# An encoder block on one core: fp16 parts for the scores, column tiles for the spatial projection, and a later spreading of x's factor

## The chip, the core and the metric

The kernel runs on one core of a Trainium2 chip. Five engines work side by side, each through its own queue in order: TensorE (PE, with the weight loads shown apart as PEld), VectorE (DVE), ScalarE (ACT), GpSimd (POOL) and SyncE (SP), which issues most of the transfers. The metric is the device time of one execution in microseconds. The kernel before takes 721.9 us, the median of three runs (721.56 to 724.05).

## The reference

One layer on 1024 tokens of width 1024, batch 1, all in float32 (cut to what the change touches):

```python
h = rmsnorm(x, norm_gain)
q, k, v, gate_a, u_in, v_in, gate_b, g_merge = jnp.split(h @ w_in, IN_SPLITS, axis=-1)
q = axial_rope(rmsnorm(q.reshape(B, S, 8, 64), q_gain), row_ang, col_ang)   # 8 query heads
k = axial_rope(rmsnorm(k.reshape(B, S, 2, 64), k_gain), row_ang, col_ang)   # 2 key heads
attn = block_attention(q, k, v) * silu(gate_a)      # softmax(q k / 8) v, both directions
u = gelu(u_in)
vv = layernorm(gelu(v_in), ln_v_gain, ln_v_bias).reshape(B, 8, 128, 8, 64)
v_mix = einsum('gij,bcjgd->bcigd', w_spatial, vv) + b_spatial.T[:, :, None]
gm = u * v_mix.reshape(B, S, 512) * silu(gate_b)
g = sigmoid(g_merge + b_merge)
out = rmsnorm(x + (g[0] * (attn @ w_proj_attn) + g[1] * (gm @ w_proj_gmlp)) @ w_out, final_gain)
```

## The kernel before

Every large product is made from split operands: an operand is written as hi + lo, and a product as three matmuls, hi·hi, hi·lo and lo·hi (`mm3`, L181 to L184). Some operands are split into two fp32r halves (`split`, L125 to L127: a copy on ACT, a subtraction on DVE), others are scaled and split into two fp16 halves (`split16`, L291 to L293).

The work goes in stages. First x arrives and k, v and the value half of the gated branch are projected (tiles `kv`, and `v` in four groups of two token blocks, `v_group`). Then, for each of 8 token blocks of 128, the layer norm (`v_post`) and the spatial projection (`spatial`): four slices of 256 columns of w_spatial, each by `mm3` with the block's fp32r halves as the stationary operand, into a PSUM tile `sp`; two copies on ACT (L398) pick out the half of the rows that is wanted for each of the two channel groups of a slice. In between come the query projection (`q_group`, tile `q`), the normalisation and rotation of q and k on DVE (`q_norm`, `rope`), their split into halves (`q_split` into `qs`, `khl` for k) and their transposes on PE (`qtp`, `ktp`), which ACT and DVE copy out of PSUM into `qT` and `kT`. A query block's `qs` holds hi in the first 64 of each 128 values and lo in the other 64, so that one transposed tile holds both halves as rows.

Attention is 64 pieces `scores(j, qt, h)`: four matmuls into a PSUM tile `s` (L626, L627, the query tile is the stationary operand), a row maximum on DVE (`nm`, L629), the exponential on ACT (`P`, L633), a reciprocal, the fp16 halves of the probabilities (`p`, ACT L639 and DVE L640), and a transfer that transposes them into `T`. `mix2` multiplies T by v on two column tiles of 64 (L654, tile `o`): two neighbouring matmuls write the lower and upper 64 rows of the output. Between the pieces stand the projections of u and of the two gates (`run_fill`, tiles `u`, `ga`, `gb`, L560 to L562). After the last piece come the projections `yb` (from `gm`), the merge gates `g`, the projections `y` and the output product `out`.

`scales` squares and sums a weight block (ACT L344, after a load of 256 KB into one of four buffers `wraw`) to get its scale; the result goes through a small PE product (`us...`), ACT and POOL. The factor 1/rms of x is spread over the partitions by 8 small products (`rb`, L271) and copied to `rB` (L274), which `norm_part` and `x_chunk` use.

The order is set twice: a list at the end of the function, written out as calls, says in which order the steps are recorded; from it a scheduler sets the final order on each engine. PSUM has three buffers for the large tiles (`S`) and one each for `o` and `z`.

Of the kernel before, what the change touches and what calls it, by code (L numbers as in the profile page):

```python
# [30 lines left out]
def hybrid_block_kernel(  # L31
# [342 lines left out]
    def v_post(c):  # L374
# [13 lines left out]

    def spatial(c):
        vh, vl = vhl[c]  # L390
        pt = ps_s(f"sp{c}")
# [4 lines left out]
        for g2 in range(2):
            rows = slice(64 * g2, 64 * g2 + 64)
            act.copy(vm[rows, :, C(c)], p3[rows, :, C(g2)])  # L398

# [37 lines left out]
    def q_split(tt):  # L437
        if True:
            g, k = tt // 2, tt % 2
            q4 = qsts[g].rearrange("p (t h d) -> p t h d", h=8, d=64)  # L440
# [1 line left out]
            act.copy(qs[:, :, 0:64], q4[:, k])
            dve.tensor_tensor(out=qs[:, :, 64:128], in0=q4[:, k], in1=qs[:, :, 0:64].bitcast(F32), op=ALU.subtract)
            full = ps_s(f"qtp{tt}") if QTP[g] == "s" else None
            for hh in range(2):
                if full is not None:
                    pt = full[:, H(hh)]
                else:
                    pt = {"o": ps_o, "z": ps_z, "S": ps_s}[QTP[g][hh]](f"qtp{tt}{hh}")
                for h in range(4):  # L450
                    pe.transpose(pt[:, C(h)].bitcast(F32R), qs[:, 4 * hh + h, :], identr)
# [99 lines left out]
    def v_affine(t):  # L551
        m3 = vm[:, t, :].rearrange("p (c i) -> p c i", i=128)
        dve.scalar_tensor_tensor(out=m3, in0=m3, scalar=cs[:, C_LNG + t:C_LNG + t + 1],
# [437 lines left out]
    load_pair(1)  # L991
    load_wsp(1)
    load_pair(2)
    early = scales(["q"] + order[:4], ["xa"] * 8)
    with tc.high_priority():
        scales_end(*early)
        qc = const([P, 2], "qc")
        dve.tensor_scalar(out=qc[:, 1:2], in0=wsc["q"][1], scalar1=2.0, scalar2=None, op0=ALU.mult)
        dve.tensor_scalar(out=qc[:, 0:1], in0=qc[:, 1:2], scalar1=qc[:, 1:2], scalar2=1.0 / 64, op0=ALU.mult, op1=ALU.mult)
    v_group(2)  # L1000
# [383 lines left out]
```

## Time and profile before

| | before |
|---|---|
| median of 3 runs | 721.9 us |
| the profiled execution | 722.31 us |
| its span, first to last instruction | 720.5 us |
| mean granted TensorE clock | 0.993 |
| PE busy | 696.2 us, 97% |
| DVE busy | 575.5 us, 80% |
| ACT busy | 455.2 us, 63% |
| POOL busy | 117.1 us, 16% |

Busy time of a matmul runs from its start to its modelled end, so neighbouring matmuls overlap; how fast PE takes them is read from the distance of two starts in the timeline. In the rows of the windows, a line gives a stretch of the span, then the busy time of each engine with its instructions, the granted clock (PEclk), the share of the DMA engines and their rate. In the rows of waits, the three numbers are the sum in us, the count and the longest.

### The profile page before, as it was taken

The page shows a single profiled execution, that of the slowest core. Times are in us where ns is not written, and L with a number is a line of the kernel's source. Part 1 is how long each engine was busy: PE and PEld are TensorE (multiplying, and loading weights), DVE is VectorE, ACT ScalarE, POOL GpSimd, SP SyncE. Part 2 cuts the span into 40 slices and gives each one's busy share as a digit, 9 for nine tenths or more (in the row PEclk, how much of TensorE's full clock was granted, in tenths as well). Part 3 has the DMA queues.
Part 4 walks back from the last instruction along what each step waited for, and adds up shares of the span by engine and source line. Part 5 has one row for each costly group of instructions (what it writes and reads, how often), then busy time and mean ns, then how long its engine had stood idle before and what let it go on. Part 6 is the DMA issues. An engine that isn't in the chain of part 4 may idle for free.

```text
span 720.5 us, 11891 instructions
## 1 busy us (share of the span) xinstructions
PE 696.2 (97%) x4625; PEld 461.9 (64%) x4625; DVE 575.5 (80%) x820; ACT 455.2 (63%) x810; POOL 117.1 (16%) x106
## 2 busy tenths in 40 slices
PE   8999999799899999999999999999999999999996
PEld 8888666455466556566656786644464557488885
DVE  6489988789898998988788899978897899953223
ACT  6775796787788977896776577545474544721011
POOL 0024224045020101011100093011012020000000
PEclk9999999999999999999999999999999999999999
DMA  8993244625689996999799630310120125330202
GB/s 295 402 405 117 89 132 134 203 37 110 117 136 189 217 183 128 187 187 178 137 202 206 193 102 15 132 72 3 41 106 1 58 88 176 116 118 12 106 30 87
DMA packets 157512, 98.18 MB, mean 136 GB/s; under 512 B 135952, under 2 KB 136592, under 8 KB 157456
## 3 DMA queue, kind: packets, MB, share of 16 engines
q1 hardware_dynamic: 156016, 92.95, 51.0%
q10 hardware_dynamic: 1440, 4.47, 1.6%
q8 instruction: 36, 0.59, 0.3%
q14 instruction: 20, 0.16, 0.1%
HBM read 59.65 MB, written 4.19 MB: 89 GB/s over the span
## 4 chain that ended last, share of the span: by engine, by line
PE 60%; DVE 14%; DMA 11%; ACT 8%; issue 4%; POOL 1%; SPq 1%; POOLq 0%; ACTq 0%; DVEq 0%
PE out L182 4%; PE out L183 4%; PE out L184 4%; DMA wraw<-in_wall_dram 4%; DMA T<-p 3%; DMA xraw<-in_xT_dram 3%; PE o L654 3%; PE g L182 3%; PE g L184 3%; PE g L183 3%; DVE p L640 3%; DVE nm L629 3%; PE s L626 2%; PE s L627 2%; PE yb L182 1%
## 5 line engine op out<-in xcount | busy, mean ns | idle before, releaser
L640 DVE SCALAR_TENSOR_TENSOR p<-P,ri,p 128x1024 f16<-128x1024 f32 x64 | 83.4, 1306 | 18.6 <-ACT p L639 18.2
L633 ACT ACTIVATE P<-s,nm 128x1024 f32<-128x1024 f32 x64 | 71.1, 1110 | 20.2 <-DVE nm L629 15.4
L639 ACT ACTIVATE p<-P,ri 128x1024 f16<-128x1024 f32 x64 | 73.0, 1142 | 10.8 <-DVE ri L636 5.8
L629 DVE TENSOR_REDUCE nm<-s 128x1 f32<-128x1024 f32 x64 | 77.4, 1212 | 1.2 <-PE s L627 1.1
L626 PE MATMUL s<-kT,qT 128*128 128x512 f32 x128 | 57.2, 447 | 8.2 <-ACT P L633 4.3
L654 PEld LDWEIGHTS <-vS 128*64 128x64 f16 x1536 | 45.1, 110 | 15.4 <-issue 13.1
L654 PE MATMUL o<-T,vS 128*64 128x128 f16 x1536 | 49.9, 220 | 3.7 <-DMA T<-p 3.6
L627 PE MATMUL s<-kT,qT 128*128 128x512 f32 x128 | 51.6, 403 | 0.0
L285 POOL TENSOR_SCALAR scg<-scg 128x1 f32<-128x1 f32 x8 | 18.8, 2348 | 181.1 <-ACT usg L284 181.1
L927 ACT ACTIVATE sq<-xr 128x1024 f32<-128x1024 f32 x7 | 7.4, 1062 | 63.5 <-DVE xr L1314 63.2
L1314 DVE TENSOR_TENSOR xr<-out,xr 128x1024 f32<-128x1024 f32 x7 | 8.6, 1225 | 45.9 <-PE out L184 45.7
L183 PE MATMUL out<-wo,yhl 128*128 128x512 f32 x96 | 37.5, 390 | 0.0
L182 PE MATMUL out<-wo,yhl 128*128 128x512 f32 x96 | 37.4, 392 | 0.0
L184 PE MATMUL out<-wo,yhl 128*128 128x512 f32 x96 | 37.3, 390 | 0.0
L182 PE MATMUL g<-x,wg 128*128 128x512 f16 x96 | 36.4, 379 | 0.0
L184 PE MATMUL g<-x,wg 128*128 128x512 f16 x96 | 36.4, 379 | 0.0
L183 PE MATMUL g<-x,wg 128*128 128x512 f16 x96 | 36.4, 379 | 0.0
L626 PEld LDWEIGHTS s<-kT,qT 128*128 128x128 f32 x128 | 24.8, 194 | 17.2 <-ACT P L633 5.5
L627 PEld LDWEIGHTS s<-kT,qT 128*128 128x128 f32 x128 | 24.9, 195 | 4.5
L182 PE MATMUL yb<-gm,wh 128*128 128x512 f32 x64 | 25.2, 394 | 0.0
L560 PE MATMUL u<-x,wu 128*128 128x512 f16 x64 | 24.3, 380 | 0.9 <-ACT s1b L357 0.6
L182 PE MATMUL v<-nh,xhl 128*128 128x512 f32 x64 | 25.1, 392 | 0.0
(547 smaller groups left out, 2016.1 us busy)
## 6 DMA issues: line engine op xcount, KB each, us to landing
wraw<-in_wall_dram SPq DMA_DIRECT2D x75, 256.0 KB, 3.4
graw<-in_wall_dram SPq DMA_DIRECT2D x16, 512.0 KB, 4.8
xraw<-in_xT_dram SPq DMA_DIRECT2D x13, 512.0 KB, 6.6
xn<-in_x_dram SPq DMA_DIRECT2D x8, 512.0 KB, 7.9
xp<-in_xT_dram SPq DMA_DIRECT2D x8, 512.0 KB, 8.2
xr<-in_x_dram SPq DMA_DIRECT2D x8, 512.0 KB, 3.7
wor<-in_wall_dram SPq DMA_DIRECT2D x8, 512.0 KB, 4.7
out_dram<-xr SPq DMA_DIRECT2D x7, 512.0 KB, 2.6
```

Source lines behind the costliest of these rows:

```text
L182: pe.matmul(o, ah, bh, start=start, stop=False)
L183: pe.matmul(o, ah, bl, start=False, stop=False)
L184: pe.matmul(o, al, bh, start=False, stop=stop)
L285: pool.tensor_scalar(out=sc[:, 1:2], in0=sc[:, 1:2], scalar1=1.0, scalar2=1e-30, op0=ALU.mult, op1=ALU.add)
L560: pe.matmul(o, wh, x16[dt][:, 0, H(h)], start=(dt == 0), stop=False)
L626: pe.matmul(sp[:, H(hf)], qs, kT[v][:, 0, H(hf)], start=True, stop=False)
L627: pe.matmul(sp[:, H(hf)], qs, kT[v][:, 1, H(hf)], start=False, stop=True)
L629: dve.tensor_reduce(out=nm, in_=sp, axis=AX.X, op=ALU.max, negate=True)
L633: act.activation(Pt, sp, AF.Exp, bias=nm, accum_out=rsum)
L639: act.activation(hi, Pt, AF.Copy, scale=ri)
L640: dve.scalar_tensor_tensor(out=lo, in0=Pt, scalar=ri, in1=hi, op0=ALU.mult, op1=ALU.subtract)
L654: pe.matmul(ot[64 * h:64 * h + 64, C(k)], vS[:, kt, v, 64 * vl:64 * vl + 64], T[:, h, 8 * p + kt, :], start=(n == 0), stop=(n == len(parts ...
```

## The change

What it does:

- **Scores.** `qs`, `khl`, `qT` and `kT` become fp16 (hi and lo halves of fp16 each), and the transposes use an fp16 identity and fp16 PSUM tiles. So that q and k lie in the range of fp16, the gains of q and k are rescaled by a common factor, made from their largest values by a few small steps on DVE and one on POOL (`gsz`).
- **Spatial projection.** w_spatial is scaled and split into fp16 halves (`wsw`), with a scale made as for the other weights: ACT squares both halves of it (into `wss`), a small PE product (`uswsp`), an ACT copy, three POOL steps, then `split16`. The normalised block is split into fp16 halves (`vhl`). `spatial` now takes two token blocks at once: for each of them 4 slices x 3 products x 2 channel groups, each with 64 stationary columns and 128 moving ones; the two channel groups are written to the lower and upper 64 rows of the PSUM tile, as in `mix2`. One ACT copy for both blocks takes the place of four. The scale is undone in `v_affine` (`lgs`).
- **Spreading of x's factor.** The products `rb` and their copies to `rB` are recorded after the first `v_group`, without priority, and no longer ahead of it.
- **The list.** Many calls stand in another order. On PE, `rb` still follows the 18 last matmuls of the first `v` group in both kernels, and the sums of the number of large matmuls are the same but for the 96 `sp` matmuls of 256 columns, which become 192 of 128 columns on column tiles.

```diff
-    rB = t4("rB", "rB")
-    with tc.high_priority():
-        rp = [ps_z("rb0"), ps_o("rb1")]
...
-        vh = sb.tile([P, 512], F32R, tag="wh", bufs=3, name=f"vh{c}")
-        vl = sb.tile([P, 512], F32R, tag="wl", bufs=3, name=f"vl{c}")
-        split(vh, vl, g, act)
-        vhl[c] = vh, vl
-
-    def spatial(c):
-        vh, vl = vhl[c]
-        pt = ps_s(f"sp{c}")
-        for t in range(4):
-            r = slice(256 * t, 256 * t + 256)
-            mm3(pt[:, r], vh[:, C(t)], vl[:, C(t)], wsh[:, r], wsl[:, r], True, True)
-        p3 = pt.rearrange("p (k i) -> p k i", k=4)
-        for g2 in range(2):
-            rows = slice(64 * g2, 64 * g2 + 64)
-            act.copy(vm[rows, :, C(c)], p3[rows, :, C(g2)])
+        vhl[c] = sb.tile([P, 2, 512], F16, tag="wh", bufs=3, name=f"vhl{c}")
+        split(vhl[c][:, 0], vhl[c][:, 1], g, act)
+
+    def spatial(k):
+        pt = ps_s(f"sp{k}")
+        for i in range(2):
+            v = vhl[2 * k + i]
+            for t in range(4):
+                for n, (a, b) in enumerate(((0, 0), (0, 1), (1, 0))):
+                    for g2 in range(2):
+                        o = 128 * t + 64 * g2
+                        pe.matmul(pt[64 * g2:64 * g2 + 64, 512 * i + 128 * t:512 * i + 128 * t + 128], v[:, a, o:o + 64],
+                                  wsw[:, b, 2 * 128 * t + 128 * g2:2 * 128 * t + 128 * g2 + 128],
+                                  start=(n == 0), stop=(n == 2))
+        act.copy(vm[:, :, 256 * k:256 * k + 256].rearrange("p t (c i) -> p t c i", c=2),
+                 pt.rearrange("p (c t i) -> p t c i", c=2, t=4))
...
-            qs = t4("og", f"qs{tt}", F32R).rearrange("p (h d) -> p h d", d=128)
+            qs = t4("og", f"qs{tt}", F16).rearrange("p (h d) -> p h d", d=128)
             act.copy(qs[:, :, 0:64], q4[:, k])
-            dve.tensor_tensor(out=qs[:, :, 64:128], in0=q4[:, k], in1=qs[:, :, 0:64].bitcast(F32), op=ALU.subtract)
+            dve.tensor_tensor(out=qs[:, :, 64:128], in0=q4[:, k], in1=qs[:, :, 0:64], op=ALU.subtract)
...
-                    pe.transpose(pt[:, C(h)].bitcast(F32R), qs[:, 4 * hh + h, :], identr)
+                    pe.transpose(pt[:, C(h)], qs[:, 4 * hh + h, :], identh)
...
-        split(wsh[:, H(h)], wsl[:, H(h)], raw, act)
+        act.activation(wsw[:, h].bitcast(F32), raw, AF.Square, accum_out=wss[:, h:h + 1])
+
+    def scale_wsp():
+        nscale.append("wsp")
+        pt = ps_oz(len(nscale), "uswsp")
+        pe.matmul(pt[:, 0:2], mscale.broadcast_to([P, P]), wss, start=True, stop=True)
+        sc = sb.tile([P, 2], F32, tag="sc", bufs=3, name="scwsp")
+        act.activation(pt[:, 8:10], pt[:, 0:2], AF.Copy, accum_out=sc[:, 1:2])
+        pool.tensor_scalar(out=sc[:, 1:2], in0=sc[:, 1:2], scalar1=1.0, scalar2=1e-30, op0=ALU.mult, op1=ALU.add)
+        pool.tensor_tensor(out=sc[:, 0:1], in0=sc[:, 1:2], in1=mhalf[:, 0:1], op=ALU.pow)
+        pool.tensor_tensor(out=sc[:, 1:2], in0=sc[:, 1:2], in1=sc[:, 0:1], op=ALU.mult)
+        for h in range(2):
+            split16(wsw[:, 0, H(h)], wsw[:, 1, H(h)], wsr[h], sc[:, 0:1], "dve")
+        dve.tensor_scalar(out=lgs, in0=cs[:, C_LNG:C_LNG + 4], scalar1=sc[:, 1:2], scalar2=None, op0=ALU.mult)
...
-                pe.transpose(pt[:, C(2 * s + k)].bitcast(F32R), khl[s][:, C(2 * t2k + k)], identr)
+                pe.transpose(pt[:, C(2 * s + k)], khl[s][:, C(2 * t2k + k)], identh)
...
     v_group(0)
+    rB = t4("rB", "rB")
+    rp = [ps_z("rb0"), ps_o("rb1")]
+    for tt in range(NT):
+        pe.matmul(rp[tt // 4][:, C(tt % 4)], rstdh[:, tt:tt + 1].broadcast_to([P, P]), identr.bitcast(F32),
+                  start=True, stop=True)
+    for h in range(2):
+        dve.tensor_copy(rB[:, H(h)], rp[h])
     v_group(1)
...
+    gsz = const([P, 4], "gsz")
+    for i in range(2):
+        dve.tensor_reduce(out=gsz[:, i:i + 1], in_=gq[:, 128 * i:128 * i + 64], axis=AX.X, op=ALU.max,
+                          apply_absolute_value=True)
+    dve.tensor_scalar(out=gsz[:, 2:3], in0=gsz[:, 0:1], scalar1=gsz[:, 1:2], scalar2=1e-30, op0=ALU.mult, op1=ALU.max)
+    pool.tensor_tensor(out=gsz[:, 2:3], in0=gsz[:, 2:3], in1=mhalf[:, 0:1], op=ALU.pow)
...
+    kT4 = sb.tile([P, 4, 1024], F16, tag="X", bufs=8, name="kT")
+    kT = [kT4[:, 2 * v:2 * v + 2] for v in range(2)]
...
+    qT2 = [sb.tile([P, 2, 2, 1024], F16, tag="qT", bufs=4, name=f"qT{i}") for i in range(2)]
+    qT = [qT2[j // 2][:, j % 2] for j in range(4)]
```

**How the built program moves.** Three places follow, each as the built program of the kernel before and of the changed one has it (line, operation, out<-in, shape; "x2" stands for two alike; numbers tell buffers apart).

The first is ACT just ahead of the first copies of transposed queries, without which the first score cannot start. Before:

```order
L442 CAST qs_1242<-qst_1048 128x8x64
L442 CAST qs_1259<-qst_1048 128x8x64
L398 COPY vm<-sp_1414 64x4x128 x2
L344 ACTIVATE wraw_2078,ssa_2075<-wraw_2078 128x512
L344 ACTIVATE wraw_2081,ssa_2075<-wraw_2081 128x512
L344 ACTIVATE wraw_2084,ssa_2075<-wraw_2084 128x512
L344 ACTIVATE wraw_2087,ssa_2075<-wraw_2087 128x512
L344 ACTIVATE wraw_2101,ssb_2098<-wraw_2101 128x512
L344 ACTIVATE wraw_2104,ssb_2098<-wraw_2104 128x512
L344 ACTIVATE wraw_2107,ssb_2098<-wraw_2107 128x512
L344 ACTIVATE wraw_2110,ssb_2098<-wraw_2110 128x512
L453 CAST qT_863<-qtp_1245 128x2x128
```

and in the changed kernel, where L338 is the square, L447 the copy of queries, L392 the copy of `sp`:

```order
L338 ACTIVATE wraw_1953,ssb_1950<-wraw_1953 128x512
L338 ACTIVATE wraw_1956,ssb_1950<-wraw_1956 128x512
L535 COPY qst_1444<-q_1395 128x1024
L447 COPY qT_941<-qtp_1319 128x2x128 x2
L447 COPY qT_942<-qtp_1326 128x2x128 x2
L436 CAST qs_1352<-qst_1065 128x8x64
L338 ACTIVATE wraw_1959,ssb_1950<-wraw_1959 128x512
L338 ACTIVATE wraw_1962,ssb_1950<-wraw_1962 128x512
L338 ACTIVATE wraw_1976,ssa_1973<-wraw_1976 128x512
L392 COPY vm<-sp_1446 128x4x256
L338 ACTIVATE wraw_1979,ssa_1973<-wraw_1979 128x512
L436 CAST qs_1369<-qst_1225 128x8x64
```

Eight squares, each of a freshly loaded weight block, stood ahead of the first copies of queries; now two do. The last copy of `sp`, which stood ahead of the eight, now has five of the squares ahead of it.

The second is DVE around the first row maximum. Before:

```order
L553 SCALAR_TENSOR_TENSOR vm<-vm,cs,bsp 128x1024 x4
L443 TENSOR_TENSOR qs_1322<-qst_1191,qs_1322 128x8x64
L629 TENSOR_REDUCE nm_1485<-s_1480 128x1
L406 TENSOR_REDUCE qf_1657<-qtmp_1655 128x16
L142 TENSOR_SCALAR qf_1657<-qf_1657,qc 128x16
L629 TENSOR_REDUCE nm_1529<-s_1524 128x1
```

and in the changed kernel (L561 is `v_affine`, L437 the query split, L637 the row maximum):

```order
L561 SCALAR_TENSOR_TENSOR vm<-vm,lgs,bsp 128x1024 x4
L437 TENSOR_TENSOR qs_1369<-qst_1225,qs_1369 128x8x64
L437 TENSOR_TENSOR qs_1614<-qst_1225,qs_1614 128x8x64
L637 TENSOR_REDUCE nm_1575<-s_1570 128x1
L400 TENSOR_REDUCE qf_1677<-qtmp_1675 128x16
L637 TENSOR_REDUCE nm_1602<-s_1597 128x1
```

The four `v_affine` steps, which need the last copy of `sp`, stand ahead of the first row maximum in both; one more query split stands there now.

The third is ACT where the scale of w_spatial is taken up, in the changed kernel alone (L485 copies the small product, L286 makes the fp16 halves, L334 squares the blocks of the first scales):

```order
L465 ACTIVATE vst_513<-v_529,rstd 128x512 x2
L485 ACTIVATE uswsp,scwsp<-uswsp 128x2
L286 ACTIVATE wsw<-wspr_601,scwsp 128x512
L286 ACTIVATE wsw<-wspr_647,scwsp 128x512
L286 ACTIVATE x_921<-xp_662,gs 128x1024
L334 ACTIVATE squ_641,ssq<-squ_641 128x1024
L286 ACTIVATE x_944<-xp_662,gs 128x1024
L334 ACTIVATE sqb_644,ssq<-sqb_644 128x1024
```

On POOL the three steps between the second row and the third stand behind the power of 16 values for k (L146 there, L143 before):

```order
L375 TENSOR_SCALAR rs_743<-mv_741 128x1
L375 TENSOR_SCALAR rs_805<-mv_803 128x1
L376 TENSOR_TENSOR rs_743<-rs_743,mhalf 128x1
L376 TENSOR_TENSOR rs_805<-rs_805,mhalf 128x1
L146 TENSOR_TENSOR kf<-kf,mhalf 128x16
L486 TENSOR_SCALAR scwsp<-scwsp 128x1
L487 TENSOR_TENSOR scwsp<-scwsp,mhalf 128x1
```

The two fp16 halves of w_spatial and the squares behind them now wait for POOL; before, the split of w_spatial came some twenty ACT steps earlier and waited for no scale.

More of the change, by code (lines that the diff above doesn't have):

```diff
@@ L21 @@
 PSCALE = 32768.0
+QKMAX = 32768.0
 VSCALE = 16384.0
@@ L473, in hybrid_block_kernel @@
     vhl = {}
-    wsh = t4("og", "wsh", F32R)
-    wsl = t4("og", "wsl", F32R)
+    wsw = t4("og", "wsw", F16, (P, 2048)).rearrange("p (k c) -> p k c", k=2)
+    wss = const([P, 2], "wss")
+    lgs = const([P, 4], "lgs")
     wsr = []
@@ L552, in v_affine @@
         m3 = vm[:, t, :].rearrange("p (c i) -> p c i", i=128)
-        dve.scalar_tensor_tensor(out=m3, in0=m3, scalar=cs[:, C_LNG + t:C_LNG + t + 1],
+        dve.scalar_tensor_tensor(out=m3, in0=m3, scalar=lgs[:, t:t + 1],
                                  in1=bsp[:, None, C(t)].broadcast_to([P, 8, 128]),
@@ L990, in hybrid_block_kernel @@
     Ak, Bk = (heads(t) for t in tabk)
[L991 to L1000, printed above, removed]
+    load_wsp(0)
     v3 = vn.rearrange("p (t e) -> p t e", e=128)
@@ L1007, in hybrid_block_kernel @@
                       apply_absolute_value=True)
-    norm_part(1)
-    prep_q(0)
-    v_group(3)
-    bias_term(0)
-    v_post(1)
-    spatial(1)
-    norm_part(0)
-    prep_q(1)
     ktmp = t4("vS", "ktmp")
     head_norm(kn, ktmp, 0, 8, "kf")
-    prep_q(2)
+    load_pair(1)
+    early = scales(["q"] + order[:4], ["xa"] * 8)
+    load_wsp(1)
+    scale_wsp()
+    load_pair(0)
+    load_pair(2)
+    with tc.high_priority():
+        scales_end(*early)
+        qc = const([P, 2], "qc")
+        dve.tensor_scalar(out=qc[:, 1:2], in0=wsc["q"][1], scalar1=2.0, scalar2=None, op0=ALU.mult)
+        dve.tensor_scalar(out=qc[:, 0:1], in0=qc[:, 1:2], scalar1=qc[:, 1:2], scalar2=1.0 / 64, op0=ALU.mult, op1=ALU.mult)
+    prep_q(0)
+    v_group(2)
+    norm_part(0)
+    v_post(0)
+    v_group(3)
+    v_post(1)
+    prep_q(1)
+    bias_term(0)
+    norm_part(1)
+    norm_part(5)
     with tc.high_priority():
@@ L1102, in hybrid_block_kernel @@
     v_affine(2)
+    scores(*hs[1])
     q_split(3)
-    scores(*hs[1])
     scores(*hs[2])
@@ L1121, in hybrid_block_kernel @@
     v_affine(3)
+    q_split(7)
+    v_affine(1)
     run_fill(*halves[0])
     q_split(6)
-    q_split(7)
+    scales(order[8:10])
+    scales(order[10:12])
     scores(*hs[12])
-    v_affine(1)
+    v_affine(0)
     mix2(*hs[0][:2])
+    scores(*hs[13])
+    scores(*hs[14])
+    prep_next()
     mix2(*hs[4][:2])
-    scales(order[10:12])
-    scales(order[8:10])
-    run_fill(*halves[1])
-    prep_next()
-    scores(*hs[13])
-    v_affine(0)
-    scores(*hs[14])
     prep_next()
@@ L1145, in hybrid_block_kernel @@
     scores(*hs[20])
+    scores(*hs[21])
     prep_next()
-    scores(*hs[21])
     mix2(*hs[12][:2])
@@ L1167, in hybrid_block_kernel @@
     scores(*hs[30])
+    scores(*hs[31])
     run_fill(*halves[11])
-    scores(*hs[31])
+    run_fill(*halves[12])
     scores(*hs[32])
@@ L1172, in hybrid_block_kernel @@
     mix2(*hs[24][:2])
-    run_fill(*halves[12])
     scores(*hs[34])
```

150 lines of the change are left out of this document (73 added, 77 removed).

## The prediction, made before the changed kernel ran

> **What bounds the kernel now.** I read the page first, then the windows stage by stage, then PE's waits, then the timeline where they stand.
>
> ```profile
> PE 696.2 (97%) x4625; PEld 461.9 (64%) x4625; DVE 575.5 (80%) x820; ACT 455.2 (63%) x810; POOL 117.1 (16%) x106
> ...
> 43.40:141.40 98.00, 93.48 (x495) 64.65 (x495) 89.27 (x140) 72.36 (x129) 29.25 (x27) 1.00 0.47 162
> 141.40:247.10 105.70, 98.47 (x871) 62.64 (x872) 94.40 (x130) 87.25 (x168) 25.30 (x20) 0.97 0.72 134
> 247.10:379.40 132.30, 130.37 (x1321) 80.91 (x1320) 113.28 (x144) 105.56 (x184) 13.79 (x10) 1.00 0.95 172
> 379.40:442.00 62.60, 62.43 (x441) 47.08 (x441) 57.88 (x82) 40.57 (x73) 22.06 (x4) 1.00 0.57 147
> 442.00:720.50 278.50, 271.97 (x1239) 170.51 (x1236) 196.55 (x283) 118.47 (x209) 23.76 (x36) 0.99 0.21 74
> ```
>
> The last five rows are A (values and queries, to 141.4), B (first part of attention, to 247.1), C (the rest of it, to 379.4), D (to the first merge gate) and E. PE is the bound in C, D and E (130.37 of 132.30, 62.43 of 62.60). In B it isn't alone: PE is busy 98.47 of 105.70 and DVE 94.40, so a PE that gets shorter by more than some 7 us there meets DVE, and the 0.97 shows a stretch of slower clock. The change's operations lie in A, B and C; D and E keep all their matmuls and start earlier by what the others save.
>
> ```profile
> PE s L626 <- ACT qT L453: 3.9, 1, 3.9
> ...
> 132.32 0.63 ACT L344 ACTIVATE wraw<-wraw 128x512 f32<-128x512 f32 x1
> ...
> 136.33 0.63 ACT L344 ACTIVATE wraw<-wraw 128x512 f32<-128x512 f32 x1 [2.06 <-DMA wraw<-in_wall_dram]
> ...
> 140.30 0.63 ACT L344 ACTIVATE wraw<-wraw 128x512 f32<-128x512 f32 x1 [0.69 <-DMA wraw<-in_wall_dram]
> ...
> 141.05 1.20 ACT L453 CAST qT<-qtp 128x256 fp32r<-128x256 f32 x4
> ...
> 147.72 1.11 ACT L633 ACTIVATE P<-s,nm 128x1024 f32<-128x1024 f32 x1
> ```
>
> The longest wait of PE in attention, 3.9 us before the first score, is not a lack of speed: ACT stands in line behind eight squares of weight blocks, 132.32 to 140.9, of which some wait for transfers; the copies of the transposed queries come only behind them.
>
> ```profile
> 142.49 0.63 PE L626 MATMUL s<-kT,qT 128*128 128x512 f32 x1
> 142.91 0.63 PE L627 MATMUL s<-kT,qT 128*128 128x512 f32 x1
> ...
> 136.97 1.27 DVE L553 SCALAR_TENSOR_TENSOR vm<-vm,cs,bsp 128x1024 f32<-128x1024 f32 x1
> 142.79 0.69 DVE L443 TENSOR_TENSOR qs<-qst,qs 128x512 fp32r<-128x512 f32 x1 [4.54 <-ACT qs L442]
> ...
> 150.01 0.69 DVE L443 TENSOR_TENSOR qs<-qst,qs 128x512 fp32r<-128x512 f32 x1 [2.68 <-ACT qs L442]
> 150.62 0.16 DVE L636 RECIPROCAL ri<-ri 128x1 f32<-128x1 f32 x1
> ```
>
> The same line costs DVE 4.54 and 2.68 us, and the scores right behind PE's wait go at 0.42 us apart. [...]
>
> **The change part by part.** *Scores.*
>
> ```profile
> 263.38 0.38 PE L561 MATMUL u<-x,wu 128*128 128x512 f16 x1
> 263.59 0.38 PE L562 MATMUL u<-x,wu 128*128 128x512 f16 x1
> 263.62 0.58 PE L626 MATMUL s<-kT,qT 128*128 128x512 f32 x1
> 264.04 0.39 PE L627 MATMUL s<-kT,qT 128*128 128x512 f32 x1
> 264.27 0.39 PE L626 MATMUL s<-kT,qT 128*128 128x512 f32 x1
> ...
> 141.40:247.10 105.70, 33.34 (x107) 20.91 (x108) 30.61 (x26) 30.03 (x50) 0.97 0.72 134
> 247.10:379.40 132.30, 38.69 (x145) 26.28 (x144) 43.25 (x37) 43.21 (x72) 1.00 0.95 172
> ```
>
> The last two rows are the windows for tile s alone: 107 of the 256 score matmuls fall into B, 145 into C. An fp16 matmul of 512 columns follows its neighbour after 0.215 us (263.38 to 263.59), a score after 0.23 (264.04 to 264.27): 0.015 saved on each, 1.6 us in B and 2.2 in C. And the first score behind fp16 work holds back the next by 0.42 (263.62 to 264.04), 0.19 more than its share; behind `o` it is 0.34, as in the row of 254.67 below. By the timeline there are some 18 such entries in each of B and C, half behind `o`; at 0.15 on the mean, 2.7 us in each. fp16 behind fp16 shows none of it, so I take both away: 4.3 us in B, 4.9 in C. Bounds: cadence alone (1.6 and 2.2) to all.
>
> *Spatial projection.*
>
> ```profile
> 79.62 0.47 PE L182 MATMUL sp<-wsh,vh 128*128 128x256 f32 x1
> ...
> 82.64 0.39 PE L182 MATMUL q<-wq,x 128*128 128x512 f16 x1
> ...
> 254.67 0.51 PE L626 MATMUL s<-kT,qT 128*128 128x512 f32 x1
> 255.01 0.40 PE L627 MATMUL s<-kT,qT 128*128 128x512 f32 x1
> ...
> 255.49 0.40 PE L627 MATMUL s<-kT,qT 128*128 128x512 f32 x1
> 255.82 2.87 PE L654 MATMUL o<-T,vS 128*64 128x128 f16 x95
> 258.62 0.39 PE L560 MATMUL u<-x,wu 128*128 128x512 f16 x1
> ...
> L398 ACT COPY vm<-sp 64x512 f32<-64x512 f32 x16 | 9.3, 579 | 1.2 <-PE sp L184 1.0
> ```
>
> Two blocks take 24 matmuls from 79.62 to 82.64, 3.0 us; four such pairs 12.1. The new form, 64 stationary and 128 moving columns on two column tiles, is that of `o`: 95 in 2.80 us (255.82 to 258.62), 0.0295 each, so 192 take 5.7. The built order cuts the four bursts into nine pieces; entering one costs 0.33 instead of 0.23, and leaving about as much, so 9 x 0.23 = 2.1. Saved: 12.1 - 7.8 = 4.3 us of PE, in A. [...] Bounds: 5.9 (whole bursts) and, if the pairs did not overlap, 12.1 - 192 x 0.059 - 2.1 = -1.3. Sixteen copies of 0.58 on ACT become four of at most 1.16 (twice the values each): 5 us less on ACT, which is not the bound in A (72.36 of 98).
>
> *Transposes.*
>
> ```profile
> 133.80 0.98 PE L451 MATMUL qtp<-identr,qs 128*128 128x128 f32 x8
> 134.62 0.39 PE L184 MATMUL q<-wq,x 128*128 128x512 f16 x1
> ```
>
> Eight take 0.82, 0.10 each. In fp16 I bound one from above by that, from below by 0.06 (128 columns, a pair of `o`): 0 to 2.6 us for the 64, most in B; I take 1.5. The copies out of them keep their size.
>
> *Scales.* DVE gains the steps of `gsz` and `lgs`, seven or so at about 0.16 (the row of 150.62): 1.1 us. ACT gains two squares, and its two halves of w_spatial now wait for POOL:
>
> ```profile
> 56.42 4.95 POOL L143 TENSOR_TENSOR kf<-kf,mhalf 128x16 f32<-128x16 f32 x1 [6.07 <-DVE kf L142]
> ...
> L356 PE MATMUL usq<-ssq,mscale x8: 173/253/254, 67.4 to 68.1; 128*128 128x5 f32 x8
> L285 POOL TENSOR_SCALAR scg<-scg 128x1 f32<-128x1 f32 x8 | 18.8, 2348 | 181.1 <-ACT usg L284 181.1
> ```
>
> POOL is free at 61.4; its three small steps end at 63 to 65 (a small one lasts up to 2.35). Two halves, two splits of x and the two last squares, at 0.65 to 1.25 each on ACT, then end at 69 to 71, and `usq`, due on PE at some 68.6 (67.4 before, and five matmuls of `v` later in the new order) with 42 matmuls of `v` behind it, waits 0 to 2.5. I take 0.5. The later `rb` costs and saves nothing: it keeps its place on PE.
>
> *The sum.* In A PE ends its queries 4.3 us earlier; the 3.9 us of waiting go too, since only two squares stand ahead of the first copies. But what then sets the pace is DVE: without its 4.54 and 2.68, less 1.1 of new work, the row maxima start 6.1 us earlier at best, and not at all if the last copy of `sp`, now behind five squares, keeps `v_affine` waiting as the queries were kept. It is five squares instead of eight, so nearer the upper end: 4.5, less 0.5 for `usq`, 4.0. In B PE loses 4.3 + 1.5 = 5.8 and DVE has some 7 us of other idle time to give; bounds 0 and 5.8, I take 4, since both would have to be dense for all of it. In C DVE is busy 113.28 of 132.30, so PE's 4.9 pass whole (3 to 4.9). Together 12.9 us: 722.3 (the profiled execution, 1.8 above its span) less 12.9 is 709.4; the median shown is 0.4 below it, so **709 us**.
>
> D can keep what the others give, but not more:
>
> ```profile
> 446.30 0.74 DVE L293 SCALAR_TENSOR_TENSOR wg0T<-s,scg,wg0T 128x512 f16<-128x512 f32 x1
> ...
> 447.18 0.38 PE L182 MATMUL g0T<-x,wg0T 128*128 128x512 f16 x1
> ```
>
> DVE, busy 57.88 of 62.60, finishes a gate's weights at 447.04 and PE uses them at 447.18. If attention ends earlier for PE than for DVE, PE waits here.
>
> **The rivals.** *PE alone counts* (chance 0.20). PE's savings, 4.3 + 3.9 + 5.8 + 4.9, and 2 us of slow clock pass whole: 20.9, so 701. For it: 97% busy. Against: DVE's 94.40 in B and the pair of rows just shown.
>
> *DVE takes the place of the waits* (0.14). The row maxima start no earlier, B stays at its length, only C gives 4.9 less 1.1: 718. For it: DVE ties with PE in B and D. Against: its idle time at 138 to 150 comes from ACT's line alone.
>
> *fp16 or the column tiles don't act as the nearest rows say* (0.04): scores keep their entries and `sp` pairs run one by one; A gives 2, B 2, C 2.2: 715.5.
>
> *Slower: the last copy of `sp`* (0.06). It stands behind five squares that wait for transfers; `v_affine`, 4 x 1.27, two query splits and the first row maximum stand behind it on DVE, and the first exponential behind that. PE, at its first score near 133, runs out of PSUM tiles after three scores and 21 other matmuls (33 at 0.215, near 140) and stands until that exponential. Before, it came at 147.72. From a copy later than about 147, which puts the exponential at 156, this eats all other gains and brings slow clock: 726. Eight squares took 8.5 us before, so five would have to take more than a dozen.
>
> **How the numbers follow.** The forecast's own case, 703 to 716, has 0.56. The range takes in PE alone at its lower end and DVE at its upper one: 699 to 719. A measurement of this kernel can tell about 0.5% from no change, 718.3 to 725.5. Faster: 0.56 + 0.20 + 0.04 + somewhat under half of 0.14, 0.86. Slower: 0.06. Within: 0.08.
>
> **What would show it.** Scores in the profile after at 0.215 with no longer step at entries; `sp` bursts near 0.03 a matmul; the first score at 133 to 136 without a wait for the query copies and without slow clock; A to the last query 4 us shorter; B with DVE over 92% busy; C shorter by 4 to 5. The prediction is wrong if PE shows a new wait of several us in B (for exponentials, or at `usq`), if DVE's idle time in B stays at 11, or if PE waits at the merge gates in D.

## The result, and the profile after

| | before | after |
|---|---|---|
| median of 8 runs each | 722.6 us | 718.0 us (715.6 to 720.1) |
| ratio, with its 95% interval | | 0.993 (0.991 to 0.995) |
| the profiled execution | 722.31 us | 718.27 us |
| its span | 720.5 us | 716.5 us |

The change makes the kernel 0.7% faster, some 4.6 us; the forecast was 13, with a range of 699 to 719. The direction is right, the size a third of it. The lines of the page, after:

```profile
span 716.5 us, 12060 instructions
...
PE 689.4 (96%) x4723; PEld 430.9 (60%) x4723; DVE 575.8 (80%) x828; ACT 450.9 (63%) x804; POOL 103.6 (14%) x110
...
PE 46%; DVE 23%; DMA 12%; ACT 10%; issue 5%; POOL 2%; SPq 1%; POOLq 0%; DVEq 0%; ACTq 0%
```

The last line is the chain that ended last, by engine. The same line of before:

```profile
PE 60%; DVE 14%; DMA 11%; ACT 8%; issue 4%; POOL 1%; SPq 1%; POOLq 0%; ACTq 0%; DVEq 0%
```

PE is still busy 96% of the time, but its share of that chain fell from 60 to 46%, and DVE's rose from 14 to 23. Now the stages, each kernel cut at the same five events: the first score, the first score of piece 33, the first merge gate's product behind the last `yb`, the last gate product (`g7T`), the end. Before, and then after:

```profile
0.00:141.40 141.40, 132.94 (x757) 100.72 (x757) 113.41 (x184) 103.41 (x181) 32.21 (x36) 1.00 0.62 222
141.40:265.60 124.20, 116.97 (x1036) 73.77 (x1037) 111.99 (x151) 102.79 (x195) 27.83 (x22) 0.98 0.77 141
265.60:441.80 176.20, 174.09 (x1595) 116.75 (x1594) 153.37 (x204) 130.38 (x228) 33.31 (x12) 1.00 0.80 162
441.80:628.80 187.00, 187.00 (x866) 100.77 (x866) 163.48 (x245) 102.21 (x185) 19.40 (x28) 1.00 0.21 74
628.80:720.50 91.70, 85.17 (x374) 69.85 (x372) 33.27 (x40) 16.45 (x25) 4.36 (x8) 0.98 0.19 75
```

```profile
0.00:137.80 137.80, 131.32 (x863) 95.47 (x864) 111.65 (x191) 101.92 (x183) 35.59 (x40) 0.99 0.64 229
137.80:258.70 120.90, 112.02 (x1030) 59.54 (x1028) 112.04 (x153) 98.61 (x187) 27.21 (x22) 0.97 0.81 142
258.70:434.30 175.60, 171.81 (x1595) 105.57 (x1593) 152.76 (x201) 130.03 (x227) 20.91 (x12) 1.00 0.80 163
434.30:623.30 189.00, 187.65 (x866) 100.45 (x866) 166.07 (x248) 103.88 (x187) 15.53 (x28) 1.00 0.21 73
623.30:716.50 93.20, 86.61 (x374) 69.84 (x372) 33.33 (x40) 16.44 (x25) 4.37 (x8) 0.98 0.20 73
```

Each stage holds the same products of PE in both kernels, but for a few transposes and small products. The length of the stages changes by -3.6, -3.3, -0.6, +2.0 and +1.5 us. In the second, DVE is now as busy as PE (112.04 and 112.02 of 120.90), with a slightly lower granted clock (0.97, before 0.98). The last two, whose matmuls the change doesn't touch, became longer. PE's waits after:

```profile
PE o L662 <- DMA T<-p: 5.3, 6, 1.9
PE ga L568 <- DVE uw L590: 3.0, 1, 3.0
PE s L634 <- ACT P L641: 2.7, 2, 1.5
PE q L186 <- DVE wq L287: 2.1, 1, 2.1
PE vabT L1050 <- DVE bsp L499: 1.3, 1, 1.3
PE usb L350 <- DVE uw L590: 1.2, 1, 1.2
...
PE g0T L187 <- DVE wg0T L287: 0.9, 2, 0.6
PE y00T L185 <- DVE ya L744: 0.5, 1, 0.5
```

The wait of 3.9 for the query copies is gone. But all rows of this view together make 20.3 us, where before they made 17.6: without that wait, 13.7 became 20.3. The new rows are waits for DVE.

### The profile page after: what moved, and what is told of

It reads as the page before. It is cut to its first block, busy times and chain, and to the rows that moved or that the text cites. A ratio compares the mean times of both kernels' runs of the same rounds, so it can differ in the third digit from the quotient of the medians.

```text
span 716.5 us, 12060 instructions
## 1 busy us (share of the span) xinstructions
PE 689.4 (96%) x4723; PEld 430.9 (60%) x4723; DVE 575.8 (80%) x828; ACT 450.9 (63%) x804; POOL 103.6 (14%) x110
## 4 chain that ended last, share of the span: by engine, by line
PE 46%; DVE 23%; DMA 12%; ACT 10%; issue 5%; POOL 2%; SPq 1%; POOLq 0%; DVEq 0%; ACTq 0%
PE out L187 4%; PE out L185 4%; PE out L186 4%; DMA T<-p 4%; DVE p L648 4%; DMA xraw<-in_xT_dram 4%; DVE nm L637 3%; ACT p L647 3%; PE g L185 3%; PE g L187 3%; PE g L186 3%; DMA wraw<-in_wall_dram 2%; PE o L662 2%; ACT P L641 2%; DMA xn<-in_x_dram 1%
## 5 line engine op out<-in xcount | busy, mean ns | idle before, releaser
L637 DVE TENSOR_REDUCE nm<-s 128x1 f32<-128x1024 f32 x64 | 77.4, 1212 | 1.8 <-PE s L635 1.7
L634 PE MATMUL s<-kT,qT 128*128 128x512 f16 x128 | 48.6, 380 | 2.8 <-ACT P L641 2.7
L635 PE MATMUL s<-kT,qT 128*128 128x512 f16 x128 | 48.5, 379 | 0.0
L279 POOL TENSOR_SCALAR scg<-scg 128x1 f32<-128x1 f32 x8 | 4.6, 581 | 201.3 <-ACT usg L278 161.9
L186 PE MATMUL q<-wq,x 128*128 128x512 f16 x64 | 24.8, 390 | 2.1 <-DVE wq L287 2.1
L186 PE MATMUL yb<-gm,wh 128*128 128x512 f32 x64 | 25.2, 394 | 0.0
L185 PE MATMUL yb<-gm,wh 128*128 128x512 f32 x64 | 25.1, 393 | 0.0
L286 ACT ACTIVATE wg<-graw,scg 128x512 f16<-128x512 f32 x16 | 11.5, 722 | 21.5 <-PE g L187 11.4
```

Of the source, the lines that this page charges most:

```text
L185: pe.matmul(o, ah, bh, start=start, stop=False)
L186: pe.matmul(o, ah, bl, start=False, stop=False)
L286: act.activation(hi, raw, AF.Copy, scale=sc)
L634: pe.matmul(sp[:, H(hf)], qs, kT[v][:, 0, H(hf)], start=True, stop=False)
L635: pe.matmul(sp[:, H(hf)], qs, kT[v][:, 1, H(hf)], start=False, stop=True)
L637: dve.tensor_reduce(out=nm, in_=sp, axis=AX.X, op=ALU.max, negate=True)
```

## Experiments

Theory D: PE's shorter work turns into waits, because DVE (or the chain of a piece through DVE and ACT) sets the pace. Theory P: PE sets it, and the waits are a small rest. The table collects what each run gave: the ratio of its time to the kernel before with its interval, in its profile the start of the last query product, of the first score of piece 33 and of the last `yb` product, and the sum of PE's waits.

| kernel | ratio (95%) | last q | piece 33 | last yb | waits |
|---|---|---|---|---|---|
| before | 1 | 137.2 | 265.7 | 441.6 | 17.6 |
| the change | 0.993 (0.991, 0.995) | 137.7 | 258.8 | 434.1 | 20.3 |
| consts_moved | 0.991 (0.990, 0.993) | 138.1 | 259.9 | 433.8 | 21.0 |
| pe_less_early | 1.000 (0.998, 1.002) | 137.9 | 264.2 | 440.0 | 27.4 |
| pe_less_late | 0.995 (0.993, 0.997) | 139.0 | 258.9 | 433.1 | 22.3 |
| dve_less_early | 0.999 (0.998, 1.001) | 138.8 | 261.9 | 438.4 | 22.5 |
| dve_less_late | 0.999 (0.997, 1.000) | 138.5 | 259.8 | 438.5 | 21.1 |
| old_with_fp16_scores | 1.000 (0.999, 1.001) | 137.0 | 264.7 | 441.0 | 24.7 |
| old_with_fp16_spatial | 1.001 (1.000, 1.002) | 138.9 | 266.1 | 441.4 | 21.7 |
| old_with_both_parts | 0.997 (0.996, 0.998) | 141.8 | 261.7 | 436.2 | 21.3 |
| new_with_fp32r_scores | 1.008 (1.006, 1.011) | 140.2 | 261.7 | 444.8 | 19.6 |
| uw_on_act | 1.002 (1.001, 1.004) | 138.2 | 262.3 | 437.3 | 23.6 |
| rb_mult_on_pool | 0.991 (0.989, 0.993) | 137.5 | 258.2 | 432.1 | 22.9 |
| four_on_pool | 0.999 (0.997, 1.001) | 142.6 | 267.6 | 441.6 | 25.0 |
| both_mends | 0.988 (0.986, 0.990) | | | | |
| both_mends_again | 0.992 (0.990, 0.994) | 138.4 | 258.3 | 432.0 | 22.0 |
| mixes_one_later | 1.000 (0.999, 1.002) | 138.0 | 264.0 | 441.1 | 25.8 |
| vab_in_other_bank | 1.002 (1.001, 1.004) | 144.1 | 266.6 | 441.0 | 26.1 |

The profiled one of both_mends' five executions took 1800.7 us, the other four 712.7 to 714.8, so its places are left empty; both_mends_again is the same kernel.

Each place is from one execution. consts_moved has the instructions of the change in the same order on PE, DVE and ACT, and rb_mult_on_pool those of both_mends_again. Within these two pairs the last query product differs by 0.4 and 0.9, the first product with v by 2.3 and 2.6, piece 33 by 1.1 and 0.1, the last `yb` by 0.3 and 0.1. Smaller differences between two rows show nothing. The change was timed in one set of runs and the other kernels in later ones, each beside the kernel before; consts_moved and rb_mult_on_pool, whose intervals overlap with that of the change, are not shown to be faster than it.

**The last stage: an address.**

```diff
-    wss = const([P, 2], "wss")          # ahead of load_wsp
-    lgs = const([P, 4], "lgs")
...
     gsz = const([P, 4], "gsz")
+    wss = const([P, 2], "wss")
+    lgs = const([P, 4], "lgs")
```

> The changed kernel with its two new small constants (wss and lgs) taken from the pool a little later, so that the large tiles behind them (yhl, the moving operand of out, among them) start 64 bytes lower; nothing else is changed, the instructions and their order are the same on every engine. The changed kernel's out matmuls follow each other after 231 to 236 ns where the kernel before had 226 to 227. Theory address: this comes from where wo and yhl lie to each other; out's 384 matmuls go back to about 227 ns, the span from the first y to the last out from 255.4 to about 253.8, the time falls by 1.5 (0.2%). Theory other (clock, writes of the output): the steps stay at 231 to 236.

The view of tile `out` by line (number, shortest, middle and longest duration in ns, first and last start), of before, after and this kernel:

```profile
L182 PE MATMUL out<-wo,yhl x17: 389/389/582, 628.9 to 640.0; 128*128 128x512 f32 x17
```

```profile
L185 PE MATMUL out<-wo,yhl x24: 393/396/580, 623.4 to 639.6; 128*128 128x512 f32 x24
```

```profile
L185 PE MATMUL out<-wo,yhl x27: 387/389/586, 621.9 to 639.8; 128*128 128x512 f32 x27
```

With the two constants elsewhere a matmul lasts 389 ns again, and the time from the last gate product to the last `out` is 84.8 us, as before, where the change had 86.2. So 1.4 us of the missing gain came from where tiles lie in memory: the change's new small constants stand between two groups of large tiles and moved the second by 64 bytes, relative to the first. Why the distance matters, no run here tells; that it does is shown, since nothing else differs. The other profiles bear it out: from the first to the last `out` there are 110.4 to 110.5 us in all seven kernels without these two constants at that place, and 112.0 in all ten with them.

**Less work for one engine.** The second product of each score left out, in the first 16 pieces or in pieces 32 to 47; or the row maximum taken over half the columns, in the same pieces.

```diff
-            pe.matmul(sp[:, H(hf)], qs, kT[v][:, 1, H(hf)], start=False, stop=True)
+            (n < 16) or pe.matmul(sp[:, H(hf)], qs, kT[v][:, 1, H(hf)], ...)    # or 32 <= n < 48
```

```diff
-        dve.tensor_reduce(out=nm, in_=sp, axis=AX.X, op=ALU.max, negate=True)
+        dve.tensor_reduce(out=nm, in_=sp[:, 0:512] if n < 16 else sp, ...); (n < 16) and dve.tensor_scalar(out=nm, in0=nm, scalar1=-60.0, ...)
```

> The changed kernel without the second of each pair of score matmuls (the product with the low half of k) in the first 16 pieces: 32 matmuls, 6.9 us of PE at 0.216. The low half of k is left out of these scores. Theory D (from the first query products at 80 to about 170 DVE sets the pace of the changed kernel, and PE's savings turn into waits and slow clock): the eight pieces before 170 give nothing, the other eight at most 3.5, so the first product with v starts where it did (169.7, within 1.5) and the time falls by 0 to 3.5, to 715 to 718. Theory P (PE sets the pace everywhere, the waits are a small rest): the first product with v comes 3.5 us earlier and the time falls by 6.9, to 711.

> The same matmuls left out in pieces 32 to 47 instead, where PE was dense. Both theories: the last yb product comes 6 to 7 us earlier (434.1 to about 427.5). Theory D adds that DVE stands at the merge gates, so the first merge gate's weights come late there and 1 to 4 us of it are given back before the first y product: 712 to 715. Theory P: all of it passes, 711.

> The changed kernel with the row maximum of the first 16 pieces taken over half of the 1024 columns (and 60 taken off, so that nothing overflows): 0.6 us less on each, 0.15 more for the subtraction, some 7 us less of DVE. Theory D: PE's wait of 3.0 for the first u's release at 158 and the slow clock behind it (2.75) go, the first product with v comes 4 to 7 us earlier, the time falls by 4 to 7, to 711 to 714. Theory P: nothing, within 1.5 of 718.

> The same shortened row maxima in pieces 32 to 47. Both theories: PE is dense there, so the last yb product comes at most 1.5 us earlier (the waits of 1.2, 0.7 and 1.4 for exponentials and transfers at 309 to 323 may go: by 3 at most), and the time stays within 3 of 718.

Neither theory foresaw this. Without 6.9 us of PE's work in the early pieces the kernel became slower than the change, and PE's waits rose from 20.3 to 27.4, by 7.1: what PE no longer did, it waited. The first product with v did come 4.8 us earlier (164.9), though 2.3 of that came in consts_moved too, without any such edit; and piece 33 came 5.5 later. In the late pieces, where PE had been called dense, 6.9 us less work brought the last `yb` only 1.0 forward; one wait there grew long:

```profile
PE o L662 <- DMA T<-p: 6.2, 6, 1.5
PE s L634 <- ACT P L641: 6.0, 3, 3.8
```

7 us less of DVE early moved the first product with v by 7.5 us (162.2), but mostly by another order: 23 products of `ga`, 5.0 us, which the change has ahead of it, stand behind it here. Piece 33, with as many products of u and the gates ahead of it as in the change, came 3.2 later all the same. With less DVE late the last `yb` came 4.4 later; from piece 33 to there PE ran the same products, but took 174.6 us of its own time for them instead of 171.6, at a clock of 0.98 instead of 1.00. So in these kernels neither less work of PE nor less of DVE brought the end forward by what it saved. A reservation holds for these four: the scheduler plans the order anew for each kernel, and it set some 70 to 430 of PE's rows elsewhere. A part of each loss may be the other order.

**The parts alone.** Scores in fp16 alone, or the spatial projection alone, or both, put into the kernel before with its written order; and the changed kernel with its scores put back to fp32r.

```diff
-            qs = t4("og", f"qs{tt}", F32R).rearrange(...)
+            qs = t4("og", f"qs{tt}", F16).rearrange(...)      # with kT, qT, khl, identh, gsz as in the change
```

```diff
-    v_post(1)
-    spatial(1)          # and spatial of 2, 4, 6 and 7 taken out
+    v_post(1)           # each pair at its later block's place; load_wsp, scale_wsp, v_post as in the change
```

> The kernel before with the scores' part of the change alone (fp16 halves of q and k, fp16 transposes, rescaled gains); spatial projection, list and spreading of x's factor as before. Theory P (PE's own time passes): scores 0.016 on 256 matmuls, 4.2, some 1.5 behind o, and 2.8 on the transposes: 8 us, 714. Theory D: the part up to score 32 is paced by DVE and gives 0 to 2, the rest 2.5: 717 to 719. The wait for the query copies of 3.9 before the first score stays in both, since the squares stay where they are.

> The kernel before with the spatial part alone: w_spatial and the normalised blocks in fp16 halves, two token blocks at once on two column tiles, one ACT copy; each pair stands in the list where its later block stood. PE gets 6 us less work before the last query product (137.2). Theory D (DVE sets when the query's operands come): the last query product stays within 1.5 of 137.2, the wait for the query copies before the first score stays, and the time within 2 of 721.6. Theory P: the last query product 4 to 6 us earlier, the time 717. A third way: the DVE work that the scale adds and moves from idle time into busy time makes PE wait longer at the queries: later than 138, 723 or more.

> The kernel before with the scores' part and the spatial part together, in the old written order (each pair of blocks at its later block's place). Alone each was worth nothing there (0.9997 and 1.001 of the time before). Theory order (PE's shorter time becomes waits unless the written order is made for it): together they are worth nothing either, 0.997 to 1.003. Theory parts (the two parts need each other, since one alone leaves PE at the same wait): 0.993 or less, as in the changed kernel.

> The changed kernel with its scores' part undone: fp32r halves of q and k, fp32r transposes, the old factor in the gain of q; spatial projection, list and scales as changed. PE gets some 8 us of work back. Theory D (PE's savings on the scores come back as waits, as they did in the kernel before with fp16 scores): the waits fall by 5 or more, the time stays within 2.5 of the changed kernel's 718. Theory P: 8 us longer, 726.

The scores alone are worth nothing, less than either theory had (714, or 717 to 719). The waits of PE in that kernel:

```profile
PE o L657 <- DMA T<-p: 7.6, 7, 2.4
PE s L629 <- ACT P L636: 5.2, 5, 2.2
PE s L629 <- ACT qT L456: 3.7, 2, 2.6
```

All rows of this view sum to 24.7, 7.1 more than before, and the span less the waits is 695.2 instead of 702.9: 7.7 us saved, 7.1 of it waited away. The spatial part alone takes `sp` from 12.7 to 6.7 us of PE, and still the last query product comes 1.7 us later: the third way came out (later than 138, 723 or more; measured 138.9 and 723.1), and not theory D, whose wait for the query copies is gone here (of the time, +0.1%, the address effect takes a share: `out` lasts 1.5 us longer in this kernel, as in the change). Both together give 0.997 in the old order, and that is with the 1.5 us at `out`. This lies at the edge of what theory order had (0.997 to 1.003) and misses theory parts (0.993 or less), but it is more than the parts alone add up to. The new written order, with the later spreading of x's factor, which no run tried alone, adds what is left to 0.993. Going back to fp32r in the new order costs 1.5%, 10 us at the last `yb` for some 8 us of PE's work; there theory P was the nearer one. Less work on PE brought little and more work cost all of it. It would look so where several engines are about equally late; but the order differs here too, and no run shows that reason.

**One wait taken away.** The copy that empties u's PSUM tile on ACT; the first eight `mix2` one piece later in the list; `vabT` in another PSUM bank (the last two on top of both mends, below).

```diff
-        dve.tensor_scalar(out=w, in0=zp, scalar1=sc, scalar2=None, op0=ALU.mult)
+        act.activation(w, zp, AF.Copy, scale=sc)
```

```diff
-    mix2(*hs[0][:2])
     scores(*hs[13])
+    mix2(*hs[0][:2])
```

```diff
-        pt = ps_o("vabT")
+        pt = ps_z("vabT")
```

> The changed kernel with the copy that empties u's PSUM tile (uw, 8 of 0.74 us) made by ACT and not by DVE. Theory D (DVE's order makes PE wait at 158): the copy of the second u comes right behind its last matmul, PE's waits for uw (3.0 at 158, 1.2 at 149) and the slow clock behind the first (2.7) go, the first product with v comes 5 to 7 us earlier. Of that, what lies behind decides: if DVE paces all of the first part, the piece of score 24 comes at most 6 us of DVE's relief in this stretch (2.2 for three copies) earlier, and the time falls by 2 or less; if PE does, by 5 to 7, to 711 to 713.

> Both mends, and the first eight products with v (mix2 of pieces 0 to 28) written one piece of scores later. PE waited 5 to 8 us in all at the first matmul of such a product for the transfer that transposes p. Theory waits (these waits are what PE's savings turned into): they fall by 2 to 4 in the part up to score 32, and the time by as much, 0.984. Theory pace (a piece becomes ready at DVE's and ACT's pace, so a wait taken away here comes back at the next exponential or fill): the part from score 0 to score 32 stays within 1 of 120.5 and the time within 2 of both mends'.

> Both mends, and the small product vabT in PSUM bank z instead of o, where it waited 1.3 us at 86 for DVE to have read the sums of w_spatial. Theory D (DVE sets the queries' operands): that wait goes, the next one, for wq at 88, grows by about as much, and the last query product stays within 0.7. Theory P: the last query product comes 1.3 us earlier and the slow clock behind the pair of waits goes too: 2 to 3 us.

All three became slower than what they started from. With `uw` on ACT the first product with v came 2.7 us earlier (167.0), less than the 5 to 7 expected and hardly more than in consts_moved (167.4), and piece 33 3.5 later. With the mixes later their waits did not shrink (7.7 us, from 4.8 in both_mends_again), and new ones came (2.5 at `o` for the copy out of the same bank). Piece 33 came 5.7 later than without the edit, but with 24 more products of u ahead of it, 5.2 us; the loss itself is the 9.1 at the last `yb`. With `vabT` elsewhere its wait (0.5 in both_mends_again) went, the wait for `wq` was 3.0 instead of 2.8, the transposes `ktp`, half of which use the same bank z, waited 3.2 instead of 0.8, and the last query product came 5.7 later, which no theory had. A wait that one takes away here is not the loss itself.

**Less work for DVE before the queries.** Two of x's eight products with `rB` on POOL; four of them, with the constants moved as well; then two of them and the moved constants together.

```diff
-    NPD = range(8)
+    NPD = tuple(i for i in range(8) if i not in (2, 6))     # or (2, 4, 6, 7)
```

> The changed kernel with the products of two of x's eight chunks with rB made by POOL and not by DVE (1.22 us each off DVE before 80). Theory D (DVE paces the queries from 80 to 98, since PE's shorter spatial pieces no longer cover it): the waits for bsp (1.3) and wq (2.1) and the slow clock behind them shrink by about 2.4 in all, the last query product comes 2 to 4 us earlier than 137.7. Rival (the waits come from the order of the list or of loads): the last query product stays within 0.7. A third way: POOL is slower than DVE and holds up the normalisation of the value blocks, PE waits longer at the first spatial piece, and the last query product comes later.

> The same with four of x's eight products on POOL (2, 4, 6 and 7), 4.9 us off DVE before 98. Theory D: the last query product and the row maxima come another 1 to 2 us earlier than with two, 0.986 of the kernel before. Rival (POOL becomes the one that is late: two halves of 1.3 us for each chunk, and the powers for the norms queue behind them): x's chunks come late, the last query product 1 us or more later than with two, 0.990 or more.

> The changed kernel with both edits that helped: the two small constants taken later (out's operands 64 bytes lower) and two of x's products with rB on POOL. The first gives 1.4 in the out stage, the second 2.1 up to the last yb product: 3.5 less than 718.0, so 714.5 in the same runs or 0.988 of the kernel before; if DVE at the merge gates takes some of it, 0.990.

> The kernel with both mends once more, for an undisturbed profile: 0.988 of the kernel before, out's matmuls at 227, the last yb product near 432, the waits at bsp and wq as with the products on POOL.

With two on POOL the last query product comes only 0.2 us earlier, as the rival had it, but the first row maximum 1.6 (138.7), and 2.0 are left at the last `yb`: 0.991. The two waits that theory D put down to DVE hardly shrank: 1.1 for `bsp` and 2.0 for `wq`, where the change had 1.3 and 2.1. With four, POOL is late (ACT waits 4.8 us for its products), the wait for `bsp` grows to 3.4, the last query product comes 5 us later, and the gain is gone, as that rival had it. Both mends gave 0.988 and, measured again, 0.992; both intervals lie below 1. That the mends add to each other isn't shown: each alone has 0.991, and the two measurements of this one kernel differ by 0.4%, as much as the gain in question.

## Why the prediction was wrong

| step | forecast | measured |
|---|---|---|
| start of attention | -4.0 | -3.6 |
| B, to piece 33 | -4.0 | -3.3 |
| C with `yb`, to the merge gates | -4.9 | -0.6 |
| gates and projections | 0 | +2.0 |
| `out` | 0 | +1.5 |
| sum, of the profiled execution | -12.9 | -4.0 |

**Cadence and entries of the scores.** The cadence is as forecast, and no first score holds back the next one:

```profile
246.28 0.38 PE L568 MATMUL u<-x,wu 128*128 128x512 f16 x1
246.50 0.38 PE L569 MATMUL u<-x,wu 128*128 128x512 f16 x1
246.72 0.38 PE L634 MATMUL s<-kT,qT 128*128 128x512 f16 x1
246.93 0.38 PE L635 MATMUL s<-kT,qT 128*128 128x512 f16 x1
247.15 0.38 PE L634 MATMUL s<-kT,qT 128*128 128x512 f16 x1
```

But the price of an entry was read wrongly. The rows from 263.38 on, which the prediction quotes, show a long step behind the first score (0.42) and a short one ahead of it: 263.59 to 263.62, 0.03. The two together are 0.45; here they are 0.22 and 0.21, 0.43. So in these rows an entry behind u cost nothing but cadence: the short step made up for the long one. Behind `o` the two steps were 0.149 and 0.335 in the middle of 15 entries and are now 0.152 and 0.226, 0.106 less. So the 5.4 us for entries were 1.4, and C had about 2.3 us of PE's work to give (173.85 us without idle time from piece 33 to the last `yb`, now 171.6), not 4.9.

**C: "PE's 4.9 pass whole".** This is the step that failed, and it failed twice. Of the 4.3 us missing here, 2.6 were never there: that is the price of the entries, and it is shown, since consts_moved, rb_mult_on_pool and both_mends_again all have 171.2 us without idle time in this stage. The other 1.7 came back as idle time of PE (2.1 before, 3.8 after). That part is less firm: consts_moved, with the same order, has 2.6 of idle time and is 2.1 shorter here than the kernel before, so most of the 2.3 can pass. pe_less_late, in another order, has a larger loss: 1.0 of 6.9 passed. PE busy 98.5% of a stage and DVE 86% did not mean that PE sets its end.

**The spatial projection and A.** The burst of 48 matmuls from 80.14 to 81.61 makes 0.031 each; `sp` fell from 12.7 to 6.6 us, more than the 4.3 taken and than the bound of 5.9 (which its own steps put at some 5.5 for whole bursts). The step into a burst was 0.31 us where the products of q ahead of it stand 0.22 apart (111.24 to 111.55); the forecast had 0.33. "In A PE ends its queries 4.3 us earlier" failed all the same: the last query product comes 0.4 us later. What PE waits for there is written by DVE. PE, and then DVE:

```profile
80.14 1.53 PE L389 MATMUL sp<-wsw,vhl 128*64 128x128 f16 x48
81.61 0.39 PE L185 MATMUL q<-wq,x 128*128 128x512 f16 x1
...
85.93 0.30 PE L1050 MATMUL vabT<-identr,vscr 128*128 128x128 f32 x1 [1.35 <-DVE bsp L499]
88.29 0.59 PE L186 MATMUL q<-wq,x 128*128 128x512 f16 x1 [2.06 <-DVE wq L287]
88.67 0.63 PE L187 MATMUL q<-wq,x 128*128 128x512 f16 x1
...
91.65 0.38 PE L185 MATMUL q<-wq,x 128*128 128x512 f16 x1
```

```profile
85.20 0.58 DVE L499 SCALAR_TENSOR_TENSOR bsp<-wsum,cs,bsp 128x128 f32<-128x128 f32 x2
...
86.31 1.26 DVE L287 SCALAR_TENSOR_TENSOR x<-xp,gs,x 128x1024 f16<-128x1024 f32 x1
87.49 1.40 DVE L287 SCALAR_TENSOR_TENSOR wq<-wraw,s0q,wq 128x512 f16<-128x512 f32 x2
```

DVE has no gap here from 75 to 96. With the shorter spatial matmuls PE waits twice, and then needs 3.36 us for eight matmuls (88.29 to 91.65, granted clock 0.50), 0.42 each, where behind them one takes 0.22. That the longer spatial ones had covered DVE's work is argued and not shown: in rb_mult_on_pool, with 2.4 us less of it, the waits stayed. The forecast saw DVE as the bound only from the row maxima on.

**The start.** The wait for the query copies went, as forecast, and there is no slow clock at that place (granted 1.00 from 137.80 to 141.00; before, 0.50 from 142.00 to 146.00); the first score came at 137.9, not at 133 to 136, and the row maxima 3.3 us earlier, where 4.0 was the sum. That the stage comes out near its forecast is in part luck: what it gained is no more than that wait of 3.9. `usq` waited 0.2. The last copy of `sp` came at 133 and kept nobody (`v_affine` waited 0.9): the slower rival did not occur.

**B.** 3.3 for 4.0: nearly right, with a wait that was named as a sign of error and came, 3.0 us for `uw` (below). This is luck in part too, since the 2.7 for entries stood in this sum as well and were some 0.7.

**D and the end.** "D can keep what the others give, but not more" was written down and priced at nothing; it took 2.0 (waits for `wg0T` and `ya` of 1.4, the rest in the steps next to them: with the waits, from the first `g0T` to the first `y` 13.98 us instead of 12.76, from the first `y00T` to the first `g` behind it 7.60 instead of 6.85), in this run. It does not follow from PE being early: from the last `yb` to the first `y`, pe_less_late lost nothing with the last `yb` at 433.1, and vab_in_other_bank 1.3 with it at 441.0. So it is no fixed price, and its cause stays open. The 1.5 at `out` was in no rival.

**The rivals.** 718 was the price of "DVE takes the place of the waits". Its time came out, though not its places: the row maxima did start earlier, and B gave more than C. PE alone (701) is refuted by the time itself. That a stand of PE brings slow clock, as the 726 of the slower rival has it, no run shows as a rule: behind the same wait of 3.01 us the steps were 0.43 us in the change and 0.22 in rb_mult_on_pool (last section). What stays open is which link sets a piece's pace between piece 16 and the last `yb`: each run that relieved one link also changed the order, so the runs show that PE's work alone does not set it, and no more.

## What to carry to other kernels

That an engine is 97% busy does not say what a saving on it is worth: here 7.7 us less of PE alone was worth nothing. Ask what the next engine can deliver at that place. A long step at a change of operand type is a price only if the step ahead of it isn't short by the same amount (here 0.42 behind and 0.03 ahead): add both. And here six small edits that took work or a wait away left the kernel 0.6 to 1.4% slower than it had been, with another order each time, so compare edits only with the order held fixed, and look at the steps of untouched stages, where a moved address shows (here 231 to 236 ns instead of 226 to 227).

## What the runs showed of the hardware

The same matmul, `out` in fp32r with 512 columns, followed its neighbour after 226 to 227 ns or after 231 to 236, depending on 64 bytes in the place of its operands; instructions and order were the same (consts_moved and the change).

The same wait of 3.01 us for `uw`, of the change, of rb_mult_on_pool and of both_mends_again:

```profile
160.91 0.59 PE L568 MATMUL ga<-x,wu 128*128 128x512 f16 x1 [3.01 <-DVE uw L590]
161.28 0.63 PE L569 MATMUL ga<-x,wu 128*128 128x512 f16 x1
161.71 0.63 PE L570 MATMUL ga<-x,wu 128*128 128x512 f16 x1
```

```profile
159.95 0.38 PE L568 MATMUL ga<-x,wu 128*128 128x512 f16 x1 [3.01 <-DVE uw L590]
160.17 0.38 PE L569 MATMUL ga<-x,wu 128*128 128x512 f16 x1
```

```profile
160.88 0.38 PE L566 MATMUL ga<-x,wu 128*128 128x512 f16 x1 [3.01 <-DVE uw L588]
161.09 0.43 PE L567 MATMUL ga<-x,wu 128*128 128x512 f16 x1
161.31 0.63 PE L568 MATMUL ga<-x,wu 128*128 128x512 f16 x1
```

In the first the matmuls behind it stand 0.43 us apart until 166.8, in the second none does, in the third they begin to after 0.2 us and end at 164.7; the granted clock from 156 to 172 was 0.79, 1.00 and 0.89. So the same wait was followed by slow steps in two of these kernels and by none in the third, and no run here tells what decides it, or whether it is one reason why the eight runs of the change lie 4.5 us apart. And slow steps did not always cost time: consts_moved has the order of the change and a clock of 0.95 where the change had 0.79 (156 to 172), and still reached piece 17 1.2 us later.
